# The last gate's 512 rows of the second output product as seven block products of their own, the sixth of them last

## The chip, the cores and the metric

One core of a Trainium2 chip runs the whole program. The time is device microseconds of one execution. Of a run with a profile there is also the span, from the first to the last instruction.

## What is computed

A trunk of two encoder layers over 512 tokens of width 1024, with 256 memory tokens. Each layer projects the normalized input, attends (the first layer with dilated windows, the second with grouped queries), attends to the memory, gates the heads, and multiplies by an output matrix of 1536 x 1024, with a residual. What matters here is the end of the second layer:

```python
        o_mem = memory_attention(q_mem, mem_h, w_mem_kv[i], mem_qn_g[i], mem_kn_g[i])
        y = jnp.concatenate([o_mix, o_mem], axis=-1) * jax.nn.silu(gate)
        x = x + jnp.einsum('bse,ed->bsd', y, w_out[i])
```

`y` is 512 tokens x 1536, `w_out[1]` is 1536 x 1024. All of it is float32.

## The kernel before

**Products of three matmuls.** TensorE takes each float32 operand as two parts, a high one (a cast by ScalarE to `fp32r`) and a low one (the source minus the high part, by VectorE). A product is high x high, low x high (`mm_early`, L176 and L177) and high x low (`mm_late`, L180).

**Seven block products.** Most large products go through `s_chunk` (L388): both operands are cut into 2 x 2 blocks, and seven products of sums of blocks (`PRODUCTS`, L386: "12", "11", "S1", "S2", "S4", "S3", "22") stand for the eight of the plain way. S1 = a21 - a22, S2 = S1 - a11, S4 = a12 + S2, S3 = a11 - a21 are made by VectorE. The weights' sums T1 to T4 are made by DMAs that add on arrival (`Weights.sum`, L277): T1 and T3 load a block on top of another one (L261), T2 adds T1 (L297), T4 adds T2 to block 21 (L307). The results are put together by `keep` (ScalarE copies a bank out of PSUM, L398) and `add` (VectorE adds a bank to a kept one, L415).

**Weights.** `PLAN` (L38) lists the weight chunks by kind, and `Weights` runs ahead of the products: SP loads a piece (128 x 1024) into a tile `wl`, ScalarE makes the high part `wh` (L323), VectorE the low part `wo` (L333). `KEEP` (L45) limits the pieces that are held at a time.

**The end of the second layer.** Three gates follow each other (`gate` in `gates`, L825); the first two make the forms of `y` for 1024 of the 1536 rows of `w_out`, the third (g = 2) makes `y` for the other 512. `out_proj` (L940) first runs the 1024 rows as seven block products of `s_chunk(512, YW, ...)`, 24 matmuls each; the attention of the second layer and the third gate's evaluation run beside the first six of them. `ev` in `out_proj` adds the residual to each quarter of the result `acc` by a DMA on POOL (L953, eight of 128 x 512). Then `out_rest` (L798) does the other 512 rows in the plain way: for each half of the columns (`n`) and each 128 tokens (`b`), twelve matmuls of 512 columns into a bank, VectorE adds the bank to `acc` (L781), and ScalarE's queue stores it (L1584). The last of these eight groups is cut into two of 256 columns (L806, L1592). In it, `y` comes as a high part cast by ScalarE (L880) and a low part by VectorE (L882); the weights are two `O1` chunks of two pieces each.

The order of the work is that of the code: a driver (`Driver`, L48) steps the generators of the evacuations and preparations at ticks between the products, and each engine works off its own queue in the order in which instructions were written.

Of the kernel before, what the change touches and what calls it, by code (L numbers as in the profile page):

```python
# [37 lines left out]
PLAN = ["W2"] + ["T2"] * 2 + ["W1", "W2s"] + ["W2" if c.isdigit() else "W1" for c in A_ORDER[1:]] + ["W2"] + ["O1"] * 2 + ["T2b"] * 2 + ["W1bs", "W2c"] + ["W1b"] * 4 + ["W2b"] + ["O1"] * 2  # L38
# [6 lines left out]
KEEP = {"T2": 8, "T2b": 6, "O1": 6, "W1": 9, "W2": 10, "W2s": 9, "W1bs": 9, "W2c": 9, "W1b": 7, "W2b": 9}  # L45
# [86 lines left out]
def trunk_kernel(ctx: ExitStack, tc: tile.TileContext, x, mem, wall, norm_g, mem_norm_g, gcol,  # L132
# [59 lines left out]
    def pieces(kind):  # L192

        return 2 * GROUPS[kind][0] if kind in GROUPS else 4 if kind in ("W1", "W1b", "W1bs") else 8

    class Weights:
        def __init__(self):
# [3 lines left out]
            for c in SEQ:  # L201
# [23 lines left out]
                else:  # L225
                    n = 1 if kind in ("W1", "W1b", "W1bs") else 2
                    at = {k: [d + i * n + x for x in range(n)] for i, k in enumerate(("21", "11", "12", "22"))}
# [162 lines left out]
    def s_chunk(n, act, ev, tokens=True, pre=None, half=False, soon=False, tight=False, place=None, pairs=False):  # L390
# [3 lines left out]
        bank, snap = [None, None], {}  # L394
# [25 lines left out]
        for i, (a, s, fresh) in enumerate(PRODUCTS):  # L420
            while a not in act:
                drv.tick()
            if fresh:
                bank[s] = [pj() for _ in range(units)]
            for x in range(units):
# [7 lines left out]

                for b, k, kk, bs, o in regions():
                    if half and b and k == per // 2:
                        n_half[0] += 1
                        if n_half[0] % half == 0:
                            drv.half()
                    st = fresh and kk == 0 and (units == 2 or b == 0)
                    if tokens:  # L440
                        mm_early(o, ah[:, kk, bs], wh[:, k], al[:, kk, bs], wh[:, k], st)
                    else:
                        mm_early(o, wh[:, k, bs], ah[:, kk], wh[:, k, bs], al[:, kk], st)
                for b, k, kk, bs, o in regions():
                    if tokens:
                        mm_late(o, ah[:, kk, bs], wo[:, k], kk == 3)
                    else:
                        mm_late(o, wo[:, k, bs], ah[:, kk], kk == 3)
                drv.free()
                W.advance()  # L450
                if x == units - 1:
# [324 lines left out]
    def out_rest(ys, acc, done, evac, last=None):  # L776
# [9 lines left out]
        for bs in ((0, 1), (2, 3)):  # L786
            for n in range(2):
# [5 lines left out]
                for b in bs:  # L793
# [4 lines left out]
                    if last and (n, b) == (1, 3):  # L798
                        assert (n, b) in done
                        for c in range(2):  # L800
                            es = slice(c * 256, c * 256 + 256)
                            for k in range(4):
                                mm_early(p[:, es], ys[k][0][:, cs], w[k][0][:, es], ys[k][0][:, cs], w[k][1][:, es], k == 0)
                            for k in range(4):
                                mm_late(p[:, es], ys[k][1][:, cs], w[k][0][:, es], k == 3)
                            V.tensor_tensor(acc[b][n][:, es], p[:, es], acc[b][n][:, es], ALU.add)  # L806
                            last(n, b, acc[b], c, es)
                            if not c:
                                drv.free()
                                drv.tick()  # L810
                        continue
# [9 lines left out]
    def gates(od, o_done, o_here, direct):  # L821
# [3 lines left out]
        def gate(H, first, g, half=False):  # L825


            yt = [[m4(F32R, "y").rearrange("p (h t) -> p h t", h=2) for _ in range(2)] for _ in range(2)] if g == 2 else None
# [3 lines left out]
            def ev(q, u, t):  # L832
# [46 lines left out]
                yield 1  # L879
                A.copy(yt[j][0][:, :, ts], tv)  # L880
# [57 lines left out]
        return gate, prep_y, YW, ys  # L938

    def out_proj(YW, ys, src, evac, tiles, half=False, last=None):  # L940
# [17 lines left out]
        out_rest(ys, acc, done, evac, last)  # L958
# [616 lines left out]
    gate, prep_y, YW, ys = gates(od_b, o_done_b, o_here_b, DIRECT_B)  # L1575
# [15 lines left out]
    def last_o2(n, b, o, c, es):  # L1591
        (nc.sync if c else nc.scalar).dma_start(ov[b][:, n * 512 + c * 256:n * 512 + c * 256 + 256], o[n][:, es])  # L1592
# [107 lines left out]
```

## Time and profile before

| | |
|---|---|
| Median of 3 runs | 945.94 us (944.49 to 946.8) |
| The profiled execution | 944.79 us |
| Its span | 943.0 us |
| Granted TensorE clock | 1.000 |
| First matmul of `out_rest` | 916.75 us from the span's start |
| Last matmuls of `out_rest` (four at L180) start | 938.95 us |
| Last addition of VectorE | 939.62 to 940.04 us |

Rows of the trace in order of time have the start in us from the span's start, the duration in us, the engine, the line of the kernel, the operation, what it writes and reads, its size and how many rows were merged (`x4`); in brackets stands how long its engine had been idle and what ended that. PE is TensorE, PEld its weight loads, DVE is VectorE, ACT is ScalarE; a q behind the name is the engine's queue, on which DMAs are issued.

### The profile page before, as it was taken

How to read it: one execution, taken by the hardware profiler on the slowest of the kernel's cores; microseconds unless marked ns; L12 is line 12 of the kernel's file. 1: busy time of each engine (PE TensorE's matmuls, PEld its weight loads, DVE VectorE, ACT ScalarE, POOL GpSimd, SP SyncE). 2: the span in 40 equal slices, each digit the busy share in tenths (PEclk: the TensorE clock that was granted, in tenths of full speed). 3: DMA queues.
4: the chain of work that ended last, by engine and by line, in shares of the span. 5: the costliest groups of instructions: out<-in, count | busy, mean ns of one | idle time of the engine just before them, and what ended most of it. 6: DMA issues, size and time to landing. Idle time of an engine off the chain costs nothing.

```text
span 943.0 us, 16294 instructions
## 1 busy us (share of the span) xinstructions
PE 935.4 (99%) x5524; PEld 823.2 (87%) x5524; DVE 790.1 (84%) x1430; ACT 682.9 (72%) x1706; POOL 339.1 (36%) x486
## 2 busy tenths in 40 slices
PE   8999999999999999999999999999999999999998
PEld 6889888888888888888889998888988999999886
DVE  6998676879888888889798999877998997789972
ACT  7775788677768686868676768547879887888860
POOL 3411425455655545464737111214253340110110
PEclk9999999999999999999999999999999999999999
DMA  9999937869786878796967989979985786784824
GB/s 348 386 267 337 289 93 188 279 135 258 159 250 144 262 152 265 158 267 135 254 172 192 262 205 249 290 253 304 277 187 113 189 232 162 209 219 109 199 41 118
DMA packets 87989, 202.96 MB, mean 215 GB/s; under 512 B 25057, under 2 KB 34529, under 8 KB 87906
## 3 DMA queue, kind: packets, MB, share of 16 engines
q1 hardware_dynamic: 68242, 139.07, 43.4%
q0 software_dynamic: 18368, 60.83, 35.0%
q10 hardware_dynamic: 1296, 2.03, 0.6%
q8 instruction: 43, 0.70, 0.3%
q14 instruction: 40, 0.33, 0.1%
HBM read 156.21 MB, written 11.08 MB: 177 GB/s over the span
## 4 chain that ended last, share of the span: by engine, by line
PE 91%; DVE 4%; DMA 3%; ACT 1%; issue 0%; POOL 0%; SPq 0%; DVEq 0%; ACTq 0%; POOLq 0%
PE pj L176 24%; PE pj L177 24%; PE pj L180 23%; DMA wl<-in_wall_dram 3%; PE qT L620 3%; PE sa L1215 2%; PE oo L1323 2%; PE pt L1302 1%; PE ptb L1529 1%; PE sa L1211 1%; PE xT L515 1%; DVE wo L333 1%; PE ob L180 1%; PE ob L177 1%; PE ob L176 1%; PE sb L171 1%
## 5 line engine op out<-in xcount | busy, mean ns | idle before, releaser
L333 DVE TENSOR_TENSOR wo<-wl,wh 128x1024 fp32r<-128x1024 f32 x255 | 312.6, 1232 | 5.5 <-ACT wh L323 5.3
L323 ACT CAST wh<-wl 128x1024 fp32r<-128x1024 f32 x255 | 268.8, 1060 | 32.2 <-PE pj L177 20.5
L176 PE MATMUL pj<-wh,hS 128*128 128x512 f32 (+1 forms) x416 | 154.5, 380 | 0.0
L177 PE MATMUL pj<-wh,hS 128*128 128x512 f32 (+1 forms) x416 | 149.0, 367 | 0.0
L176 PE MATMUL pj<-wh,h 128*128 128x512 f32 (+1 forms) x312 | 115.4, 379 | 0.0
L177 PE MATMUL pj<-wh,h 128*128 128x512 f32 (+1 forms) x312 | 111.7, 367 | 0.0
L463 POOL TENSOR_TENSOR rstd<-mse,half 128x4 f32<-128x4 f32 (+2 forms) x98 | 103.0, 1052 | 8.2
L180 PE MATMUL pj<-wo,hS 128*128 128x512 f32 (+1 forms) x416 | 99.5, 366 | 0.0
L177 PEld LDWEIGHTS pj<-wh,hS 128*128 128x128 f32 x416 | 78.8, 189 | 11.2
L176 PEld LDWEIGHTS pj<-wh,hS 128*128 128x128 f32 x416 | 78.6, 189 | 11.1 <-DVE sn L415 0.2
L180 PEld LDWEIGHTS pj<-wo,hS 128*128 128x128 f32 x416 | 72.5, 189 | 13.1
L462 POOL TENSOR_SCALAR mse<-hss 128x4 f32<-128x4 f32 (+1 forms) x88 | 46.0, 523 | 101.7 <-ACT junk L608 93.9
L608 ACT ACTIVATE junk<-sn 128x128 f32<-128x128 f32 x264 | 79.3, 310 | 3.4 <-DVE sn L409 3.3
L1159 POOL TENSOR_TENSOR ta<-sn,tabs 128x128 f32<-128x128 f32 (+1 forms) x64 | 34.7, 549 | 119.6 <-DVE sn L613 91.8
L398 ACT COPY sn<-pj 128x512 f32<-128x512 f32 x116 | 63.9, 588 | 17.7 <-PE pj L180 16.9
L180 PE MATMUL pj<-wo,h 128*128 128x512 f32 (+1 forms) x312 | 74.5, 366 | 0.0
L307 POOL DMA_DIRECT2D wl<-wl x33 | 29.3, 897 | 109.9 <-DVE wo L333 69.8
L176 PEld LDWEIGHTS pj<-wh,h 128*128 128x128 f32 x312 | 59.0, 189 | 8.4 <-DVE sn L415 0.2
L177 PEld LDWEIGHTS pj<-wh,h 128*128 128x128 f32 x312 | 59.1, 189 | 8.3
L415 DVE TENSOR_TENSOR sn<-pj,sn 128x512 f32<-128x512 f32 x87 | 59.4, 684 | 7.0 <-PE pj L180 6.7
L261 POOL DMA_DIRECT2D wl<-in_wall_dram x38 | 35.9, 963 | 75.2 <-DMA wl<-in_wall_dram 22.3
L180 PEld LDWEIGHTS pj<-wo,h 128*128 128x128 f32 x312 | 54.4, 189 | 9.7
(255 smaller groups left out, 2363.3 us busy)
## 6 DMA issues: line engine op xcount, KB each, us to landing
wl<-in_wall_dram SPq DMA_DIRECT2D x222, 512.0 KB, 7.4
wl<-wl POOLq DMA_DIRECT2D x66, 512.0 KB, 5.6
wl<-in_wall_dram POOLq DMA_DIRECT2D x42, 512.0 KB, 8.5
od<-o SPq DMA_DIRECT2D x11, 256.0 KB, 5.5
og<-od SPq DMA_DIRECT2D x10, 256.0 KB, 8.5
x<-in_x_dram SPq DMA_DIRECT2D x4, 512.0 KB, 9.2
v0d<-sn SPq DMA_DIRECT2D x8, 256.0 KB, 11.3
acc<-in_x_dram POOLq DMA_DIRECT2D x8, 256.0 KB, 7.0
```

The source lines that it names most:

```text
L176: T.matmul(o, a, b, start=start, stop=False, skip_group_check=True)
L177: T.matmul(o, c, d, start=False, stop=False, skip_group_check=True)
L180: T.matmul(o, a, b, start=False, stop=stop, skip_group_check=True)
L261: queue.dma_start(t, wall[d], **how)
L323: A.copy(wh, self.tile[self.items[i]])
L333: V.tensor_tensor(wo, self.tile[key], wh.bitcast(F32), ALU.subtract)
L398: A.copy(t, b)
L415: V.tensor_tensor(t, b, t, ALU.subtract if q == "12" else ALU.add)
L462: G.tensor_scalar(e, ss, EPS, None, ALU.add)
L463: G.tensor_tensor(r, e, half[:, 0:n], ALU.pow)
L608: A.activation(jk, p[:, j * 128:(j + 1) * 128], AF.Square, scale=by, accum_out=ss[:, j:j + 1])
L1159: G.tensor_tensor(ta[:, 0:n], xn[:, 0:n, 0:32], ropeA[:, 0, b, s0:s0 + n], ALU.mult)
```

## The change

In the second layer `out_rest` is no longer called. The third gate leaves its four blocks of `y` as they are (`forms=True`), a new generator `prep_l` makes from them the seven forms for a second `s_chunk`, over 512 rows (`K=2`, so that each product has twelve matmuls), and the two `O1` chunks become one chunk `W1o` of six loads, with sums T1 to T4. In this `s_chunk` the last two products change places: "22", the seventh, goes sixth into banks of its own (`at`), and "S3", the sixth, comes last, cut into one whole bank and two halves of the other. `mid` and `final` add both into what is stored, so that no step stands between S3 and the stores but two operations of VectorE. The functions of the first layer stay as they are.

```diff
-PLAN = [...] + ["W1bs", "W2c"] + ["W1b"] * 4 + ["W2b"] + ["O1"] * 2
+PLAN = [...] + ["W1bs", "W2c"] + ["W1b"] * 4 + ["W2b", "W1o"]
...
-                    for k in ORDER:
+                    for k in ORDER[:5] + ("T4", "T3") if kind == "W1o" else ORDER:
...
-    def s_chunk(n, act, ev, ..., pairs=False):
+    def s_chunk(n, act, ev, ..., pairs=False, K=4, tail=None):
...
+            if name == "s5" and tail:
+                tail[0](u, t)
...
+        def mid(u, b):
+            t = snap["21", u] = s2(name="sn")
+            tail[1](u, t, b)
+            yield 1
+
+        if tail:
+            after = after[:5] + ((mid,),)
-        for i, (a, s, fresh) in enumerate(PRODUCTS):
+        for i, (a, s, fresh) in enumerate(PRODUCTS[:5] + (("22", 2, True), ("S3", 1, False)) if tail else PRODUCTS):
...
-                bank[s] = [pj() for _ in range(units)]
-            for x in range(units):
+                bank[s] = [(at if s == 2 else pj)() for _ in range(units)]
+            for x in range(K // per):
...
+                if tail and i == 6:
+                    for b, c in ((0, slice(0, 512)), (1, slice(0, 256)), (1, slice(256, 512))):
+                        o, ts = bank[s][b][:, c], slice(b * 128, (b + 1) * 128)
+                        for k in range(per):
+                            mm_early(o, ah[:, k, ts], wh[:, k, c], al[:, k, ts], wh[:, k, c], False)
+                        for k in range(per):
+                            mm_late(o, ah[:, k, ts], wo[:, k, c], k == per - 1)
...
+                        tail[2](b, snap["21", b], snap["s5", b], o, c)
+                    continue
...
+                if forms:
+                    ys[2 * j + i] = t
+                    return
                 A.copy(yt[j][0][:, :, ts], tv)
...
+        def prep_l():
+
+            def put(k, src):
+                t = m4(F32R, "yl" + k)
+                A.copy(t[:, 0:512], src)
+                drv.late(lambda: V.tensor_tensor(t[:, 512:1024], src, t[:, 0:512].bitcast(F32), ALU.subtract))
+                YL[k] = t.rearrange("p (a k t) -> p a k t", a=2, k=2)
...
+            put("12", ys[2])
...
+            put("11", ys[0])
...
+            V.tensor_tensor(s1, a21, a22, ALU.subtract)
+            put("S1", s1)
+            yield 1
+            V.tensor_tensor(s2_, s1, a11, ALU.subtract)
+            put("S2", s2_)
+            yield 1
+            V.tensor_tensor(a12, a12, s2_, ALU.add)
+            put("S4", a12)
+            yield 1
+            V.tensor_tensor(a21, a11, a21, ALU.subtract)
+            put("S3", a21)
+            yield 1
+            put("22", a22)
...
-        out_rest(ys, acc, done, evac, last)
+        if not last:
+            out_rest(ys, acc, done, evac)
+            return
+        prep_l, YL = ys
+        drv.spawn(prep_l())
+
+        def ev_l(q, u, t):
...
+            V.tensor_tensor(acc[b][n], t, acc[b][n], ALU.add)
+            yield 1
+            yield from evac(n, b, acc[b])
+
+        def sum_22(u, t):
...
+            V.tensor_tensor(t, t, acc[2 + u][1], ALU.add)
+
+        def sum_21(u, t, p):
...
+            V.tensor_tensor(t, p, acc[2 + u][0], ALU.add)
+
+        def final(u, t, t22, p, c):
+            V.tensor_tensor(t[:, c], p, t[:, c], ALU.add)
+            last(0, 2 + u, t, c)
+            V.tensor_tensor(t22[:, c], t22[:, c], p, ALU.subtract)
+            last(1, 2 + u, t22, c)
+
+        s_chunk(512, YL, ev_l, tight=True, K=2, tail=(sum_22, sum_21, final))
...
-    gate, prep_y, YW, ys = gates(od_b, o_done_b, o_here_b, DIRECT_B)
+    gate, prep_y, YW, ys = gates(od_b, o_done_b, o_here_b, DIRECT_B, True)
...
+    def last_o2(n, b, t, c):
+        (nc.sync if n else nc.scalar).dma_start(ov[b][:, n * 512 + c.start:n * 512 + c.stop], t[:, c])
```

Up to the last product of the 1024 rows each queue keeps its order, but for the third gate's casts (ScalarE) and subtractions (VectorE), which are gone, and for loads and sums of weights. In what follows the lines of before and of the changed kernel differ by the change: L415 of before is L417 now, L409 is L411, L953 is L999.

VectorE at the end of the program, before, from the evacuation of the large product's last bank on (`pj` are banks of PSUM, `acc` the result with the residual, `wo` the low part of weights):

```order
L415 TENSOR_TENSOR acc<-pj,acc 128x512
L333 TENSOR_TENSOR wo<-wl,wh 128x1024
L415 TENSOR_TENSOR acc<-pj,acc 128x512
L781 TENSOR_TENSOR acc<-pj,acc 128x512
L333 TENSOR_TENSOR wo<-wl,wh 128x1024
L781 TENSOR_TENSOR acc<-pj,acc 128x512 x5
L806 TENSOR_TENSOR acc<-pj,acc 128x256
L781 TENSOR_TENSOR acc<-pj,acc 128x512
L806 TENSOR_TENSOR acc<-pj,acc 128x256
```

VectorE of the changed kernel from the same place on (`yl` and `ylS` are forms of `y` with their low part at L955, or a block sum at L970 and L973; `sn` are blocks of `y` or kept results):

```order
L417 TENSOR_TENSOR acc<-pj,acc 128x512 x2
L333 TENSOR_TENSOR wo<-wl,wh 128x1024
L955 TENSOR_TENSOR yl_11515<-sn,yl_11515 128x512
L333 TENSOR_TENSOR wo<-wl,wh 128x1024
L970 TENSOR_TENSOR yl<-sn 128x512
L955 TENSOR_TENSOR ylS_11543<-yl,ylS_11543 128x512
L417 TENSOR_TENSOR sn<-pj,sn 128x512 x2
L333 TENSOR_TENSOR wo<-wl,wh 128x1024
L973 TENSOR_TENSOR yl<-yl,sn 128x512
L955 TENSOR_TENSOR ylS_11569<-yl,ylS_11569 128x512
L333 TENSOR_TENSOR wo<-wl,wh 128x1024
L976 TENSOR_TENSOR sn<-sn,yl 128x512
```

Where one evacuation a product stood, there now stand a block sum, a low part of the form, a low part of the weights and the evacuations. The queue goes on with two L1014, the low part of S4, a low part of weights, L979, two L1020 (the additions to block 22), and then:

```order
L955 TENSOR_TENSOR ylS_11616<-sn,ylS_11616 128x512
L955 TENSOR_TENSOR yl_11623<-sn,yl_11623 128x512
L417 TENSOR_TENSOR sn<-pj,sn 128x512 x2
L1024 TENSOR_TENSOR sn<-at,acc 128x512
L1014 TENSOR_TENSOR acc<-sn,acc 128x512 x2
L1024 TENSOR_TENSOR sn<-at,acc 128x512
L1027 TENSOR_TENSOR sn<-pj,sn 128x512
L1029 TENSOR_TENSOR sn<-sn,pj 128x512
L1027 TENSOR_TENSOR sn<-pj,sn 128x256
L1029 TENSOR_TENSOR sn<-sn,pj 128x256
L1027 TENSOR_TENSOR sn<-pj,sn 128x256
L1029 TENSOR_TENSOR sn<-sn,pj 128x256
```

The low part of form 22, of which the sixth product has need, now stands behind all of this, and two operations of VectorE follow each piece of the seventh.

TensorE's last matmuls before, the two halves of the last group, with the engine whose semaphore an instruction waits for:

```order
L176 MATMUL pj<-wh,y 128x256 [waits DVE_49]
L177 MATMUL pj<-wo,y 128x256
L176 MATMUL pj<-wh,y 128x256
L177 MATMUL pj<-wo,y 128x256
L176 MATMUL pj<-wh,y 128x256
L177 MATMUL pj<-wo,y 128x256
L176 MATMUL pj<-wh,y 128x256
L177 MATMUL pj<-wo,y 128x256
L180 MATMUL pj<-wh,y 128x256 x4
```

And in the changed kernel, the last product's two half banks:

```order
L176 MATMUL pj<-wh,ylS_11616 128x256
L177 MATMUL pj<-wh,ylS_11616 128x256
L176 MATMUL pj<-wh,ylS_11616 128x256
L177 MATMUL pj<-wh,ylS_11616 128x256
L180 MATMUL pj<-wo,ylS_11616 128x256 x2
L176 MATMUL pj<-wh,ylS_11616 128x256 [waits DVE_49]
L177 MATMUL pj<-wh,ylS_11616 128x256
L176 MATMUL pj<-wh,ylS_11616 128x256
L177 MATMUL pj<-wh,ylS_11616 128x256
L180 MATMUL pj<-wo,ylS_11616 128x256 x2
```

The second half still waits for VectorE's reads of the first, and a half has six matmuls where it had twelve.

More of the change, by code (lines that the diff above doesn't have):

```diff
@@ L225, in __init__ @@
                 else:
[L226 to L227 removed]
+                    n = 1 if kind in ("W1", "W1b", "W1bs", "W1o") else 2
+                    at = {k: [d + i * n + x for x in range(n)] for i, k in enumerate(("11", "21", "12", "22") if kind == "W1o" else ("21", "11", "12", "22"))}
                     if kind == "W2c":
@@ L774, in mem_attn, with out_rest @@
                             (0, top, 1), (1, recip, 1), (4, hi, 1), (4, lo, 1), (6, out_, 1), step=step)
-    def out_rest(ys, acc, done, evac, last=None):
+    def out_rest(ys, acc, done, evac):
         def ev(n, b, p):
@@ L797, in out_rest @@
                     p = pj()
[L798 to L811, printed above, removed]
                     for k in range(4):
```

43 lines of the change are left out of this document (30 added, 13 removed).

## The prediction

> **What bounds the kernel now.** I begin with the page: the busy shares, then the chain that ended last.
>
> ```profile
> PE 935.4 (99%) x5524; PEld 823.2 (87%) x5524; DVE 790.1 (84%) x1430; ACT 682.9 (72%) x1706; POOL 339.1 (36%) x486
> ...
> PE 91%; DVE 4%; DMA 3%; ACT 1%; issue 0%; POOL 0%; SPq 0%; DVEq 0%; ACTq 0%; POOLq 0%
> ```
>
> TensorE is busy all the time and is the chain. The change touches the tail alone, so I cut the end into three stretches: most of the large output product, its last part, and the plain product of the last gate's rows (from 916.75). Columns are each engine's busy time, then granted clock, DMA share, GB/s.
>
> ```profile
> 863.00:890.00 27.00, 27.00 (x147) 23.14 (x146) 26.33 (x47) 22.87 (x43) 3.95 (x5) 1.00 0.68 139
> 890.00:916.75 26.75, 26.75 (x140) 22.70 (x140) 21.53 (x33) 19.61 (x32) 3.20 (x4) 1.00 0.34 97
> 916.75:943.00 26.25, 22.32 (x109) 18.64 (x107) 8.90 (x13) 0.34 (x1) 2.06 (x3) 1.00 0.45 120
> ```
>
> Up to 916.75 TensorE has no idle time. Behind it VectorE works 8.90 of 26.25 us and ScalarE almost nothing: that is the room into which the change puts work. Then TensorE's rows in order of time, from the last matmuls of the large product on.
>
> ```profile
> 915.84 1.07 PE L180 MATMUL pj<-wo,y 128*128 128x512 f32 x4
> 916.75 0.39 PE L176 MATMUL pj<-wh,y 128*128 128x512 f32 x1
> ...
> 919.47 0.39 PE L176 MATMUL pj<-wh,y 128*128 128x512 f32 x1
> ...
> 935.79 0.28 PE L176 MATMUL pj<-wh,y 128*128 128x256 f32 x1
> ...
> 937.89 0.39 PE L176 MATMUL pj<-wh,y 128*128 128x256 f32 x1 [0.52 <-DVE acc L806]
> 938.12 0.28 PE L177 MATMUL pj<-wo,y 128*128 128x256 f32 x1
> 938.24 0.28 PE L176 MATMUL pj<-wh,y 128*128 128x256 f32 x1
> ...
> 938.95 0.64 PE L180 MATMUL pj<-wh,y 128*128 128x256 f32 x4
> ```
>
> A group of twelve 512-column matmuls takes 919.47 - 916.75 = 2.72 us, 0.227 us each from start to start; one ends 0.39 us after its start. At 256 columns a step is 0.12 us, and the first step behind a wait 0.23. The only wait is at 937.89: the second half of the last group writes the PSUM bank whose first half VectorE still reads.
>
> VectorE's rows of the same stretch, and the last store.
>
> ```profile
> 914.25 1.29 DVE L409 TENSOR_TENSOR acc<-acc 128x512 f32<-128x512 f32 x2
> 916.49 0.69 DVE L415 TENSOR_TENSOR acc<-pj,acc 128x512 f32<-128x512 f32 x1 [0.96 <-PE pj L180]
> 917.10 1.22 DVE L333 TENSOR_TENSOR wo<-wl,wh 128x1024 fp32r<-128x1024 f32 x1
> 918.24 0.68 DVE L415 TENSOR_TENSOR acc<-pj,acc 128x512 f32<-128x512 f32 x1
> ...
> 937.42 0.42 DVE L806 TENSOR_TENSOR acc<-pj,acc 128x256 f32<-128x256 f32 x1 [3.46 <-PE pj L180]
> 937.76 0.68 DVE L781 TENSOR_TENSOR acc<-pj,acc 128x512 f32<-128x512 f32 x1
> 939.62 0.42 DVE L806 TENSOR_TENSOR acc<-pj,acc 128x256 f32<-128x256 f32 x1 [1.18 <-PE pj L180]
> ```
> ```profile
> 940.07 0.34 SPq L1592 DMA_DIRECT2D out_dram<-acc  x1
> ```
>
> One VectorE operation occupies the engine (start to start) for 0.60 us at 512 columns (916.49 to 917.10; the pair at 914.25, SBUF alone, lasts 1.29 = 0.60 + 0.69), 1.14 at 1024 (917.10 to 918.24) and 0.34 at 256 (937.42 to 937.76). The last one ends at 940.04, and the span ends 2.96 us later: store, landing, closing waits.
>
> **The change part by part.**
>
> *TensorE.* Eight groups of twelve become seven products of twelve: 12 x 0.227 = 2.72 us less.
>
> *Ahead of the tail.* Four casts on ScalarE go, each like this one from SBUF, and four subtractions on VectorE.
>
> ```profile
> 884.36 0.63 ACT L880 CAST y<-sn 128x512 fp32r<-128x512 f32 x1
> ```
>
> They lay beside a TensorE without idle time, so they are worth nothing. The large product keeps its order on TensorE, so the first of the seven products can still start at 916.75, and VectorE still starts its first evacuation of the large product's last bank at 916.49.
>
> *Behind 916.49 on VectorE.* By the order of the change it now has, in 512-column operations, 6 evacuations at L417, 6 low parts (L955; the seventh is done earlier), 4 block sums (L970 to L979), 8 additions of parts (L1014, L1020, L1024) and the 2 whole ones of the end (L1027, L1029): 26 x 0.60 = 15.6 us. Five low parts of weights are 5 x 1.14 = 5.7, four quarter pieces 4 x 0.34 = 1.4. Together 22.7 us against 8.90 before and against 19.0 us of matmuls. **VectorE becomes the bound**, so the tail has to be walked along its queue.
>
> Two of its low parts wait for ScalarE in a round trip: the block sum ends, ScalarE casts it, VectorE subtracts the cast. Such a handover is seen at the start of the program.
>
> ```profile
> 11.99 0.59 ACT L164 CAST act<-xT 128x512 fp32r<-128x512 f32 x1 [1.15 <-PE xT L515]
> ...
> 12.61 0.69 DVE L167 TENSOR_TENSOR act<-xT,act 128x512 fp32r<-128x512 f32 x1 [0.75 <-ACT act L164]
> ...
> 13.35 0.50 PE L177 MATMUL pj<-wh,act 128*128 128x512 f32 x1 [0.23 <-DVE act L167]
> ...
> 13.69 0.39 PE L176 MATMUL pj<-wh,act 128*128 128x512 f32 x1
> ```
>
> ScalarE ends at 12.58 and VectorE starts at 12.61: 0.03 us. VectorE ends at 13.30 and the matmul that needs the low part starts at 13.35: 0.05, and its next one 0.34 later instead of 0.23. So from the start of a block sum to the start of its low part: 0.69 + 0.03 + 0.63 (the cast of L880) + 0.03 = 1.38 us, 0.78 more than its slot (the way from VectorE to ScalarE taken as 0.03 too). This hits S1 and S2, whose sum and low part are neighbours in the queue; for S4 and S3 two operations stand between.
>
> The walk: from 916.49 up to the low part of form 22 stand 17 operations of 512 columns (10.2), 5 of 1024 (5.7) and two round trips (1.56): it starts at 933.95 and ends at 934.64. TensorE's sixth product waits for it at its second matmul: 934.69, next at 935.03; the bank of the first 128 tokens is complete with the tenth matmul, 7 x 0.227 later plus 0.39: 937.01. Without waits the sixth product would have started at 916.75 + 5 x 2.72 = 930.35. VectorE has meanwhile evacuated the fifth and is free from 935.75. From 937.05: L1024, two L1014, L1024 (2.4), L1027 and L1029 whole (1.2), L1027 and L1029 on the first quarter piece, the last of which starts at 940.99 and ends at 941.41.
>
> The last quarter piece of TensorE goes to the bank that these two have read, and by the order it waits for VectorE: start 941.46, six matmuls (0.23, then 4 x 0.12, then 0.28 for the last to end): 942.45. Then L1027 at 942.49, L1029 at 942.83, its end 943.25. Before, this end was 940.04: **+3.2 us**. The store behind it is of the same size as before, so 2.96 us follow again.
>
> [...] By addresses alone VectorE would run straight on (941.33 and 941.67, end 942.09), and the sum would be +2.05.
>
> Unknown costs, by bounds:
> - Two stores now stand on ScalarE's queue ahead of the cast of form 22. The group of output stores has
>
> ```profile
> L1584 ACTq DMA_DIRECT2D out_dram<-acc x7: 338/339/461, 920.4 to 938.7; - x7
> ```
>
>   so 0.7 to 0.9 us. The cast of S3 starts at 932.27 by the walk, that of 22 then at 933.0 to 933.3 and ends at 933.6 to 933.9, when VectorE wants it: 0 to 0.1 us. I take 0.
> - The weights of the last 512 rows now come as six loads, with four sums made by DMAs on POOL, T1 to T2 to T4 in series. Before, SP issued the last loads, and POOL sums landed, as follows.
>
> ```profile
> 867.08 24.92 SPq L261 DMA_DIRECT2D wl<-in_wall_dram  x7
> ```
> ```profile
> wl<-in_wall_dram SPq DMA_DIRECT2D x7, 512.0 KB, 4.1
> ...
> wl<-in_wall_dram POOLq DMA_DIRECT2D x2, 512.0 KB, 7.0
> wl<-wl POOLq DMA_DIRECT2D x1, 512.0 KB, 5.2
> ```
>
>   Seven loads end at 892.0, 3.6 us apart. Two more: 899.2 (an estimate from these rows). The T2 load, third from the end, is then out at 892.0 and landed at 896.1; T1's sum at about 899.5 (888.4 + 4.1 + 7.0), T2's at 904.7. It is cast at 916.04 at the earliest. T4 needs also the low part of block 21 (about 911.3): landed at 916.9, cast behind 921. Cost 0, with 4 us and more to spare; if the spare goes, every late us of T4 is a late us of the end.
> - The eight additions of x1d stand on POOL between these sums; the first that VectorE waits for anew is L1014 at about 928.6. Cost 0.
> - How exact is the walk? Some 35 slots at 0.60 +- 0.01 and a dozen handovers at 0.03 to 0.10: -0.4 to +0.9 us. I take 3.2 as it stands.
>
> The span goes from 943.0 to 946.2, this execution from 944.79 to 948.0. The median of the three runs is 945.94, 1.15 above the profiled execution, so the forecast for the median is 945.94 + 3.2 = **949.1 us** (+0.34%).
>
> **The rivals.**
> - *VectorE keeps up, and the saved matmuls show: faster.* Then TensorE runs through: the last piece but one is complete at 935.24, two reads of it until 936.04, the last piece 936.09 to 937.08, VectorE until 937.88: 2.2 us ahead of 940.04, **943.8**. It decides at the low part of form 22: this would have to be there by 930.35 and not 934.64, which takes 512-column slots of about 0.44 us. For it speaks that VectorE is idle for 0.96 us ahead of 916.49; against it that slots are 0.60 whether an operand is in PSUM or not, and that the queue's order leaves that work behind. Chance 0.04.
> - *The weight sums are late.* If SP gets its buffers later than I think, or the three sums in series take the double, T4 comes 2 to 5 us late: about **952.5**. For it: POOL's sums wait behind each other and behind x1d additions. Against: the spare above. Chance 0.05.
> - *The clock drops when TensorE waits.* A second slower step of 0.45 us on the matmuls of the path (seven of the sixth product, five quarter steps) adds 1.6 + 0.6: **951.3**. Against it: the granted clock is 1.00 in all stretches, and the longest new gap of TensorE is 1.9 us (939.6 to 941.46). Chance 0.03. [...]
> - The change doesn't do what it says: the order shows the twelve matmuls gone, so this is out.
>
> **How the numbers follow.** The forecast has 0.88, the rivals 0.04, 0.05, 0.03. About 0.3% (2.8 us) is what a measurement of this kernel can tell from no change. The forecast's +3.2 lies just over that bound; with its -0.4 to +0.9 and some 0.6 us for medians of runs that spread over 2.3 us, about 0.7 of its chance falls above: 0.60 slower, 0.27 within, 0.01 faster. With the rivals: 0.60 + 0.05 + 0.03 = 0.68 slower, 0.27 within, 0.01 + 0.04 = 0.05 faster. The range takes the forecast with its errors and part of the late sums: 947.2 to 951.2.
>
> **What would show it.** In the changed profile the first product of the last gate starts near 916.75; VectorE is busy nearly without idle time from there to about 935.8, with two gaps of some 0.7 us ended by ScalarE; TensorE waits in the products of S1, S2, S4 and 22, each time for VectorE or ScalarE, some 4 us in all, and some 2 us at the last piece. The stretch behind 916.75 has 22 to 23 us of VectorE. Wrong would be: waits of ScalarE for DMA ahead of a weight cast (sums late), matmul steps of 0.45 (clock), or slots of VectorE under 0.6.

## The result, and the profile after

The changed kernel takes 948.85 us (median of eight, 947.11 to 950.7), the kernel before, timed beside it, 944.71 us (median of eight, 944.31 to 946.8). The ratio is 1.004, with a 95% interval of 1.0028 to 1.0052: slower by 0.4%. The profiled execution of the changed kernel took 947.53 us, its span is 945.7 us.

First the page's busy times and chain, to be read against those of before.

```profile
PE 933.9 (99%) x5506; PEld 819.8 (87%) x5506; DVE 802.3 (85%) x1449; ACT 691.1 (73%) x1718; POOL 343.4 (36%) x490
...
PE 93%; DVE 4%; ACT 1%; DMA 1%; issue 0%; SPq 0%; DVEq 0%; ACTq 0%
```

Over 946 us hardly anything shows: 1.5 us less on TensorE, 12.2 more on VectorE, 8.2 more on ScalarE. The stretches tell more; the columns are those of before (busy time of each engine with its instructions, granted clock, DMA share, GB/s).

```profile
890.00:916.75 26.75, 26.75 (x139) 22.65 (x138) 19.86 (x29) 19.43 (x32) 7.07 (x8) 1.00 0.80 186
916.75:945.70 28.95, 20.96 (x90) 15.43 (x88) 22.49 (x35) 9.60 (x16) 1.80 (x3) 0.96 0.43 109
```

Ahead of 916.75 nothing has moved for TensorE: it is full, and with the weights' extra loads and sums the DMAs' rate nearly doubles (186 GB/s against 97). Behind it TensorE has fewer matmuls (18 less in the whole kernel: twelve, and six of the piece that is cut), and VectorE has gone from 8.90 to 22.49 us. TensorE's rows say where it waits.

```profile
916.42 0.39 PE L176 MATMUL pj<-wh,yl 128*128 128x512 f32 x1
...
921.89 0.39 PE L176 MATMUL pj<-wh,ylS 128*128 128x512 f32 x1
922.36 0.50 PE L177 MATMUL pj<-wh,ylS 128*128 128x512 f32 x1
...
925.94 0.51 PE L176 MATMUL pj<-wh,ylS 128*128 128x512 f32 x1 [0.80 <-ACT ylS L954]
926.67 0.51 PE L177 MATMUL pj<-wh,ylS 128*128 128x512 f32 x1 [0.22 <-DVE ylS L955]
...
930.22 0.50 PE L177 MATMUL pj<-wh,ylS 128*128 128x512 f32 x1 [0.52 <-DVE ylS L955]
...
933.48 0.50 PE L176 MATMUL at<-wh,yl 128*128 128x512 f32 x1 [0.48 <-ACT yl L954]
934.36 0.50 PE L177 MATMUL at<-wh,yl 128*128 128x512 f32 x1 [0.38 <-DVE yl L955]
...
936.99 0.39 PE L176 MATMUL pj<-wh,ylS 128*128 128x512 f32 x1
...
941.14 0.39 PE L176 MATMUL pj<-wh,ylS 128*128 128x256 f32 x1 [1.92 <-DVE sn L1029]
941.36 0.28 PE L177 MATMUL pj<-wh,ylS 128*128 128x256 f32 x1
```

Where before there was one wait of 0.52 us, there are now waits in the products of S2, S4 and 22, each for ScalarE's cast or VectorE's low part, and 1.92 us at the last quarter piece. The second matmul of S1's product comes 0.47 us behind the first instead of 0.23, so it waits too, without a bracket. The six products up to the last take 20.57 us (916.42 to 936.99) where six times 2.72 are 16.32: 4.2 us of waiting in all. Now VectorE, from the block sum S1 to its end.

```profile
920.24 0.69 DVE L970 TENSOR_TENSOR yl<-sn 128x512 f32<-128x512 f32 x1
921.62 0.69 DVE L955 TENSOR_TENSOR ylS<-yl,ylS 128x512 fp32r<-128x512 f32 x1 [0.69 <-ACT ylS L954]
922.22 1.28 DVE L417 TENSOR_TENSOR sn<-pj,sn 128x512 f32<-128x512 f32 x2
923.42 1.22 DVE L333 TENSOR_TENSOR wo<-wl,wh 128x1024 fp32r<-128x1024 f32 x1
924.55 0.69 DVE L973 TENSOR_TENSOR yl<-yl,sn 128x512 f32<-128x512 f32 x1
925.92 0.69 DVE L955 TENSOR_TENSOR ylS<-yl,ylS 128x512 fp32r<-128x512 f32 x1 [0.68 <-ACT ylS L954]
...
933.62 0.69 DVE L955 TENSOR_TENSOR yl<-sn,yl 128x512 fp32r<-128x512 f32 x1
934.22 1.28 DVE L417 TENSOR_TENSOR sn<-pj,sn 128x512 f32<-128x512 f32 x2
936.73 0.69 DVE L1024 TENSOR_TENSOR sn<-at,acc 128x512 f32<-128x512 f32 x1 [1.23 <-PE at L180]
...
940.67 0.41 DVE L1029 TENSOR_TENSOR sn<-sn,pj 128x256 f32<-128x256 f32 x1
942.15 0.43 DVE L1027 TENSOR_TENSOR sn<-pj,sn 128x256 f32<-128x256 f32 x1 [1.07 <-PE pj L180]
942.49 0.41 DVE L1029 TENSOR_TENSOR sn<-sn,pj 128x256 f32<-128x256 f32 x1
```

Brackets are what to look for: from the tail's start on this queue has four gaps, two round trips to ScalarE (0.69 and 0.68) and two waits for TensorE, which itself had waited for VectorE. Everything else follows start to start at 0.60, 1.14 or 0.34 us.

In what follows **the tail** is the time from the first matmul of the last gate's rows to the end of VectorE's last operation. It went from 23.29 us (916.75 to 940.04) to 26.48 (916.42 to 942.90). The span ends 2.82 us behind it (2.94 before, by the span unrounded).

### The profile page after: what moved, and what is told of

It is laid out like the page before. It is cut to its first block, busy times and chain, and to the rows that moved or that the text cites. A ratio compares the mean times of both kernels' runs of the same rounds, so it can differ in the third digit from the quotient of the medians.

```text
span 945.7 us, 16305 instructions
## 1 busy us (share of the span) xinstructions
PE 933.9 (99%) x5506; PEld 819.8 (87%) x5506; DVE 802.3 (85%) x1449; ACT 691.1 (73%) x1718; POOL 343.4 (36%) x490
## 4 chain that ended last, share of the span: by engine, by line
PE 93%; DVE 4%; ACT 1%; DMA 1%; issue 0%; SPq 0%; DVEq 0%; ACTq 0%
PE pj L176 24%; PE pj L177 24%; PE pj L180 24%; PE qT L641 3%; PE sa L1289 2%; PE oo L1397 2%; PE ptb L1603 1%; PE pt L1376 1%; PE sa L1285 1%; DVE wo L333 1%; PE xT L536 1%; PE ob L180 1%; PE ob L177 1%; PE ob L176 1%; PE sb L171 1%; PE sb L170 1%
## 5 line engine op out<-in xcount | busy, mean ns | idle before, releaser
L333 DVE TENSOR_TENSOR wo<-wl,wh 128x1024 fp32r<-128x1024 f32 x258 | 316.2, 1232 | 6.7 <-ACT wh L323 6.5
L323 ACT CAST wh<-wl 128x1024 fp32r<-128x1024 f32 x258 | 272.0, 1060 | 31.9 <-PE pj L177 20.9
L398 ACT COPY sn<-pj 128x512 f32<-128x512 f32 x122 | 67.2, 590 | 19.3 <-PE pj L180 18.5
L417 DVE TENSOR_TENSOR sn<-pj,sn 128x512 f32<-128x512 f32 x91 | 62.0, 684 | 7.1 <-PE pj L180 6.6
L261 POOL DMA_DIRECT2D wl<-in_wall_dram x40 | 38.1, 969 | 82.2 <-DMA wl<-in_wall_dram 30.1
```

The source lines that it names most:

```text
L261: queue.dma_start(t, wall[d], **how)
L323: A.copy(wh, self.tile[self.items[i]])
L333: V.tensor_tensor(wo, self.tile[key], wh.bitcast(F32), ALU.subtract)
L417: V.tensor_tensor(t, b, t, ALU.subtract if q == "12" else ALU.add)
```

## The experiments

The theory after the result is that of the prediction: VectorE's queue sets the tail, and the last wait for a bank adds to it. Its rivals are the weights' sums (late), the handovers between VectorE and ScalarE (their latency, not the slots), and the new order of the last two products. Executions of one kernel spread by 2 to 4 us here, so the verdicts go by the tail, read from each trace.

| Kernel | first matmul | tail | span behind it | time, us |
|---|---|---|---|---|
| before | 916.75 | 23.29 | 2.94 | 944.71 (8) |
| change | 916.42 | 26.48 | 2.82 | 948.85 (8) |
| no sums of weights | 917.69 | 26.47 | 2.83 | 948.77 |
| no sums of `y` | 918.57 | 23.76 | 2.83 | 946.93 |
| two sums made twice | 917.28 | 27.97 | 2.84 | 949.86 |
| usual order | 916.93 | 27.10 | 3.48 | 949.27 |
| last piece whole | 918.24 | 25.21 | 3.50 | 948.72 |
| operands early | 917.46 | 26.08 | 3.53 | 948.83 |
| additions on GpSimd | 916.07 | 29.33 | 2.84 | 950.01 |
| early, whole, GpSimd | 917.38 | 25.48 | 4.09 | 948.46 (6) |
| additions by DMA | 918.12 | 25.35 | 3.54 | 948.77 |
| early, whole, DMA | 917.59 | 22.88 | 4.24 | 945.95 (11) |
| before again | 917.32 | 23.31 | 2.95 | 945.35 |
| the same, stores earlier | 917.42 | 22.66 | 3.50 | 945.58 (11) |

Medians have their number of executions behind them, the others are one execution. Each tail is read from one profile.

**No sums of weights.** For the last chunk T1 to T4 become plain loads, or a name for one.

```diff
+            if self.sums and PLAN[self.sums[0][0][0]] == "W1o":
+                if key[1] == "T4":
...
+                    self.tile[key] = self.tile[key[0], "21", key[2]]
```

> The sums T1 to T4 of the last gate's weights are left out: the four pieces are used as they were loaded, so that the four DMAs that add are gone from POOL (the output of the last gate's rows is then not the reference's). I measure the tail, from the first matmul of the last gate's rows to the end of VectorE's last operation: 23.29 us in the kernel before, 26.48 in the changed one. Theory V (VectorE's queue is the bound): the tail stays at 26.5, within 0.1. Theory S (the sums of the weights or their DMAs come late and hold TensorE): the tail shrinks by 2 to 3 us, to 23.5 to 24.5. Theory H (the handovers between VectorE and ScalarE are the cost): 26.5.

The tail is 26.47 us, as in the change. The sums cost nothing; that rival is out.

**No sums of `y`.**

```diff
-            V.tensor_tensor(s1, a21, a22, ALU.subtract)
-            put("S1", s1)
+            put("S1", a21)
...
-            V.tensor_tensor(a12, a12, s2_, ALU.add)
             put("S4", a12)
```

> The four block sums S1, S2, S4 and S3 of the last gate's y are left out: the forms are cast from single blocks (the output of the last gate's rows is then not the reference's). Casts, low parts and everything else stay. Theory V: 4 slots of 0.60 and two round trips of 0.78 go from VectorE's queue ahead of the low part of form 22, 3.9 us; TensorE's seven products (5 x 2.72 up to the sixth) then stand close behind, so the tail shrinks by 2.7 us, to 23.8. Theory H: the two round trips go, 1.5 us: 25.0. Theory S: 26.5.

23.76: 2.72 us less, the number that was expected, but not by the way that was expected. Both round trips were to go, and TensorE was to be the bound. In the trace only S2's round trip is gone (0.78 us of the queue); the low part of S1 now waits longer for its cast, which stands behind other work of ScalarE:

```profile
923.61 0.69 DVE L955 TENSOR_TENSOR ylS<-sn,ylS 128x512 fp32r<-128x512 f32 x1 [1.13 <-ACT ylS L954]
...
933.77 0.50 PE L177 MATMUL at<-wh,yl 128*128 128x512 f32 x1 [0.52 <-DVE yl L955]
```

That is 0.44 us more than in the change (1.13 against 0.69). So four slots of 0.60 make 2.40, and the handovers together 0.34. TensorE's sixth product still waits for VectorE's low part: VectorE's queue stays the bound, and the slots are most of what counts. The theory of the handovers had 25.0.

**Two sums made twice.** One more operation ahead of S1's and S2's form each.

```diff
             V.tensor_tensor(s1, a21, a22, ALU.subtract)
+            V.tensor_tensor(s1, a21, a22, ALU.subtract)
```

> VectorE makes the block sums S1 and S2 twice, one after the other into the same tile; the result is unchanged. This adds two operations of 512 columns to VectorE's queue and no wait. Theory V: each slot ahead of the low part of form 22 is paid in full: the tail grows by 1.2 to 1.4 us, to 27.7 to 27.9. Theory S or a bound of TensorE: the tail stays at 26.5.

27.97: 1.49 us for two operations, about 0.75 each. The slot is 0.60; the repeated operation, which writes the same tile, starts 0.72 behind the first (921.10 to 921.82 in the trace), 0.12 more than a slot. Every slot ahead of form 22 reaches the end of the kernel.

**The usual order.** S3 sixth, 22 last, all of it through `add` and `keep` as in other products.

```diff
-        s_chunk(512, YL, ev_l, tight=True, K=2, tail=(sum_22, sum_21, final))
+        s_chunk(512, YL, ev_l, tight=True, K=2)
```

> The seven products of the last gate's rows in the usual order, S3 sixth and 22 last, with the usual evacuations: the second half of the change is undone, the first stays. Theory V: the work on VectorE in front of the last two products is nearly the same, but behind the last product there now stand two evacuations and four additions of the result instead of two operations, and no bank wait: by the slots the tail is 27.1 us, 0.6 longer than with 22 sixth, and 3.8 longer than before the change. Rival B (the order with the cut last product and its bank wait is what costs): the tail is shorter than 26.5, 24 to 25.

27.10 us: the changed order is worth 0.6 us, so it isn't what made the kernel slower.

**The last piece whole.**

```diff
-                    for b, c in ((0, slice(0, 512)), (1, slice(0, 256)), (1, slice(256, 512))):
+                    for b, c in ((0, slice(0, 512)), (1, slice(0, 512))):
```

> The last product's second bank comes in one piece of 512 columns instead of two of 256, so that no matmul goes to a bank that VectorE still has to read; VectorE then has two operations of 512 columns at the end instead of four of 256. Theory that the end is VectorE's queue plus one wait for the bank: VectorE's last four quarter operations (4 x 0.34) and the wait between them go, two of 0.60 come; the tail (first matmul of the last gate's rows to the end of VectorE's last operation, 26.48 us in the change, 23.29 before) becomes 25.3. Theory that VectorE is the bound in throughput alone and the order at the end costs nothing: 26.2 to 26.5.

25.21 us, 1.27 less: the wait for the bank was a cost of its own. But the span now ends 3.50 us behind VectorE instead of 2.82, with last stores twice as large and the DMAs at 377 to 385 GB/s from 943 to 945: half of the gain is given back.

**Operands early.** `prep_l` starts ahead of the large product.

```diff
+        if last:
+            prep_l, YL = ys
+            drv.spawn(prep_l())
         s_chunk(512, YW, ev, half=half, tight=True, place=place)
...
-        prep_l, YL = ys
-        drv.spawn(prep_l())
```

> The generator that makes the operands of the last products (casts, low parts, block sums) is started ahead of the first products of the other gates instead of behind them, so that its first casts and low parts run where VectorE still has idle time. Theory that VectorE's queue behind the start of the tail is the bound: whatever of it goes ahead of the start comes off the tail; by the order of the instructions that is about 1 us: 25.5. Theory that the operands' handovers (ScalarE's cast, then VectorE's low part) set the end and not the queue: 26.4, since the block sums keep their place behind each other.

26.08, between the two, so the number alone decides nothing. TensorE's rows at the last piece say why, and the stretches around it, with the granted clock third from the end.

```profile
941.09 0.58 PE L176 MATMUL pj<-wh,ylS 128*128 128x256 f32 x1 [2.93 <-DVE sn L1030]
941.48 0.42 PE L177 MATMUL pj<-wh,ylS 128*128 128x256 f32 x1
941.69 0.41 PE L176 MATMUL pj<-wh,ylS 128*128 128x256 f32 x1
```
```profile
936.00:940.00 4.00, 2.16 (x13) 1.72 (x11) 4.00 (x8) 0.00 (x0) 0.00 (x0) 1.00 0.17 66
940.00:940.80 0.80, 0.00 (x0) 0.00 (x0) 0.80 (x3) 0.00 (x0) 0.00 (x0) 0.65 0.15 59
940.80:943.00 2.20, 1.65 (x6) 1.36 (x6) 0.46 (x2) 0.00 (x0) 0.00 (x0) 0.50 0.91 336
```

TensorE now comes to the last piece earlier and waits 2.93 us for the bank, and meanwhile the granted clock falls to half. The steps are 0.39 and 0.21 us instead of 0.22 and 0.12, and from the piece's first matmul to VectorE's next operation it takes 1.69 us (941.09 to 942.78) where the change took 1.01 (941.14 to 942.15). Without these 0.68 us the tail would be 25.40, the 25.5 of the queue theory.

**Additions on GpSimd.**

```diff
-            V.tensor_tensor(acc[b][n], t, acc[b][n], ALU.add)
+            G.tensor_tensor(acc[b][n], t, acc[b][n], ALU.add)
...
-            V.tensor_tensor(t, t, acc[2 + u][1], ALU.add)
+            G.tensor_tensor(t, t, acc[2 + u][1], ALU.add)
```

> Six additions of finished parts (the four of L1014 and the two of L1020, 128x512 each) go from VectorE to GpSimd, which has 1.8 us of work in this stretch. Theory that VectorE's queue is the bound: six slots of 0.60 go from the queue, but not all stand ahead of the low part of form 22 or of the end; with GpSimd at an estimated 1.25 us for one of them (worked out from its 0.5 to 0.75 us at 64 to 128 columns) the tail becomes about 25.1. If GpSimd takes over 3 us for each, they land too late for the output and the tail stays at 26.5 or gets longer. Theory that handovers are the bound: 26.5.

29.33: neither theory had a tail 2.85 us longer. GpSimd's rows of this kernel, and VectorE's beside the first of them:

```profile
922.65 3.48 POOL L1014 TENSOR_TENSOR acc<-sn,acc 128x512 f32<-128x512 f32 x2 [4.00 <-DVE sn L417]
927.89 3.53 POOL L1020 TENSOR_TENSOR sn<-sn,acc 128x512 f32<-128x512 f32 x2 [1.76 <-ACT sn L398]
938.08 2.54 POOL L1014 TENSOR_TENSOR acc<-sn,acc 128x512 f32<-128x512 f32 x2 [6.65 <-DVE sn L417]
```
```profile
921.88 1.28 DVE L417 TENSOR_TENSOR sn<-pj,sn 128x512 f32<-128x512 f32 x2
923.08 1.94 DVE L333 TENSOR_TENSOR wo<-wl,wh 128x1024 fp32r<-128x1024 f32 x1
924.94 1.75 DVE L973 TENSOR_TENSOR yl<-yl,sn 128x512 f32<-128x512 f32 x1
927.37 0.69 DVE L955 TENSOR_TENSOR ylS<-yl,ylS 128x512 fp32r<-128x512 f32 x1 [0.68 <-ACT ylS L954]
927.97 2.31 DVE L333 TENSOR_TENSOR wo<-wl,wh 128x1024 fp32r<-128x1024 f32 x1
930.21 1.76 DVE L976 TENSOR_TENSOR sn<-sn,yl 128x512 f32<-128x512 f32 x1
```

Two additions take GpSimd 2.54 us where VectorE has little to do (busy for 1.31 of them), 1.27 each, close to the estimate of 1.25; beside VectorE they take 3.5. And VectorE's own operations, 0.69 and 1.22 us elsewhere, take 1.75, 1.94 and 2.31: four of them lose 3.9 us in all, while the four additions ahead of form 22 that left the queue were worth 2.4. All four (L333 twice, L973, L976) read two tiles of SBUF; L417, which reads one input from PSUM, keeps its 0.60 step beside the start of GpSimd's first addition (922.65, within the pair at 921.88, which takes 1.28 as elsewhere).

**All three.** The edits of the last three experiments together.

> All three edits together: last piece whole, operands made early, six additions on GpSimd. Theory that VectorE's queue is the bound: the gains add up nearly whole, the tail becomes 22.5 us (change 26.48, before 23.29), so that the seven products beat the kernel before by 0.5 to 1.1 us: 944.0 where the kernel before has 944.7. If something else bounds it once the queue is shorter (ScalarE's casts, GpSimd), the tail stays above 24 and the kernel is slower than before.

25.48 and 948.46 us (ratio to before 1.0038, 1.0025 to 1.0051): in time no better than the change (948.85), though the tail is 1.00 us shorter. VectorE's operations beside GpSimd's additions are stretched as in the run before, to 1.76 to 2.32 us, so this is the second case of its expectation.

**Additions by DMA.** To tell whether it was GpSimd's work or only the additions' lateness, the same six are left to DMAs that add.

```diff
-            V.tensor_tensor(acc[b][n], t, acc[b][n], ALU.add)
+            G.dma_start(acc[b][n], t, accum_op=ALU.add)
...
-            V.tensor_tensor(t, t, acc[2 + u][1], ALU.add)
+            G.dma_start(t, acc[2 + u][1], accum_op=ALU.add)
```

> The same six additions as in the run before with GpSimd (four of L1014, two of L1020), but made by DMAs that add into the target (issued by GpSimd, as the x1d additions of L999), so that GpSimd computes nothing. The run with GpSimd's own additions ended at a tail of 29.33 us, with VectorE's operations beside them stretched from 0.69 to 1.75 us. Theory that GpSimd's and VectorE's operations hinder each other: with DMAs VectorE's operations keep their 0.69 and 1.22 us, six slots go from its queue, and the tail becomes about 25.0 (change 26.48). Theory that the additions were late, or that their order was the trouble: the DMAs take longer than GpSimd did (4 to 5 us from issue to landing), so the tail stays at 27 or more.

VectorE's groups of this kernel in the tail, with mean ns at the end:

```profile
L333 DVE TENSOR_TENSOR wo<-wl,wh 128x1024 fp32r<-128x1024 f32 x5 | 6.1, 1216 | 0.0
...
L973 DVE TENSOR_TENSOR yl<-yl,sn 128x512 f32<-128x512 f32 x1 | 0.7, 685 | 0.0
L976 DVE TENSOR_TENSOR sn<-sn,yl 128x512 f32<-128x512 f32 x1 | 0.7, 684 | 0.0
```

The same operations are back at 1.22 and 0.69 us, the tail is 25.35 against 29.33, though a DMA takes 3.8 us from issue to landing. So it was the two engines' hindering each other, not lateness: the 3.98 us between the two tails are what the four stretched operations lost (3.9). Six slots (3.6 us) brought 1.13 against the change: with the additions gone, S4 and S3 have round trips that wait 0.69 us each, as S1 and S2, and VectorE waits 0.24 for the cast of form 22 and 0.53 for TensorE's last product.

**Early, whole, and four additions by DMA.** A trial for a version that beats both kernels.

```diff
-            V.tensor_tensor(acc[b][n], t, acc[b][n], ALU.add)
+            if q == "11":
+                G.dma_start(acc[b][n], t, accum_op=ALU.add)
+            else:
+                V.tensor_tensor(acc[b][n], t, acc[b][n], ALU.add)
```

The other edits are those shown for operands early, the whole piece, and block 22's additions by DMA.

> Operands made early, last piece whole, and four of the six additions (the first two of L1014 and the two of L1020) by DMAs that add; the last two additions of L1014 stay on VectorE, since a DMA would land them after the rest of the output. Theory that VectorE's queue is the bound: the tail becomes 22.9 us (change 26.48, before 23.29), the kernel level with the one before or up to 0.5 us faster: 944.3 to 945.5. If the DMAs disturb VectorE or the stores at the end, the tail stays above 24 and the time above 946.

The tail is 22.88, as worked out, and TensorE's waits are down to two (0.85 and 0.42 us). Yet the time is 945.95, 1.0013 of before (1.0004 to 1.0022). The stretches around VectorE's end at 940.47 show it in the last two columns, DMA share and GB/s:

```profile
937.00:940.00 3.00, 1.72 (x8) 1.10 (x6) 3.00 (x6) 0.00 (x0) 0.00 (x0) 1.00 0.37 143
940.00:943.00 3.00, 0.00 (x0) 0.00 (x0) 0.47 (x1) 0.00 (x0) 0.00 (x0) 1.00 0.99 378
```

The queue is no longer the end; the output is. Six pieces of 256 KB become ready within some 4 us, and from 940 on the DMAs move them at 378 GB/s without a pause. In the kernel before, the same output trickles out with each group of twelve matmuls (seven stores at L1584 from 920.4 to 938.7 us).

**Before again.** The kernel before, unchanged.

> The kernel before, profiled once more, for the spread of what stands ahead of the tail. The start of the last gate's products was 916.75 in the first profile of before and 916.07 to 918.57 in the changed kernels, whose code up to about 867 us is the same. Theory that the start moves from run to run by waits for DMAs of the unchanged part: here it lies anywhere in 916 to 918.6, and the tail is 23.3 again (23.2 to 23.4). Theory that the change delays the start: 916.7 again.

Tail 23.31, first matmul at 917.32. The start moves without any change. One wait that comes and goes stands in code that is the same in all kernels:

```profile
539.44 0.95 PE L1302 MATMUL pt<-ident,p 128*128 128x128 f32 x7 [0.45 <-DVE p L1289]
```

It is in this profile of before and not in the first one, and in eight of the twelve profiles of changed kernels. Compared matmul by matmul with the first profile of before, TensorE runs at a fixed distance in each of the other thirteen, within 0.05 us, from 600 us up to the first matmul of the tail. The distances, -0.67 to +1.82 us, come about in the first 150 us, at this wait and between 560 and 590 us. On all five engines the instructions and their order are the same in all kernels up to 879 us, so nothing that the change does near the end moves the start.

**The same, stores earlier.** As the trial above, with the last two additions and their stores ahead.

```diff
-            yield 1
+            if not (tail and q == "12"):
+                yield 1
             yield from ev(q, u, t)
...
                 G.dma_start(acc[b][n], t, accum_op=ALU.add)
+                yield 1
             else:
                 V.tensor_tensor(acc[b][n], t, acc[b][n], ALU.add)
-            yield 1
             yield from evac(n, b, acc[b])
```

> As the run before (operands made early, last piece whole, four additions by DMA), but the two additions of L1014 that are left on VectorE come right behind their evacuations, and their stores are issued right behind them, ahead of the last products' stores on ScalarE's queue. In the run before, VectorE ended 0.4 us earlier in its tail than in the kernel before (22.88 against 23.29), but the span went on for 4.24 us behind it (2.96 before): from 940 to 943 the DMAs moved 377 GB/s without a pause, and one store of 256 KB that was ready at 938.1 was issued at 940.29. Theory that this last stretch is bound by the rate of the output's DMAs: with that store ahead of the stretch, a quarter of a MB less is left in it, 0.69 us, the span ends 3.5 us behind VectorE's last operation, the tail stays at 22.8, and the time is 945.1 to 945.4, within 0.1% of the kernel before. Theory that the end behind VectorE is a fixed latency of the last store: 4.2 us again, 945.9.

Tail 22.66 and 3.50 us behind it, as the theory of the DMAs' rate has it; its span behind the first matmul is 26.16 us, that of before 26.23 and 26.26. The time is 945.58, 1.0009 of before (1.0000 to 1.0018), 0.2 above what was expected. That is 3.3 us under the change, and no version is faster than the kernel before.

## Why the prediction was right, point by point

- *Twelve matmuls less on TensorE, 2.72 us, and none of it gained*: so it came. Its busy time behind 916.75 fell from 22.32 to 20.96 us, and the waits, 4.2 us in the first six products (in those of S1, S2, S4 and 22, as forecast) and 1.92 at the last piece, took more back.
- *VectorE becomes the bound with 22.7 us*: 22.49 us behind 916.75. Taking its sums out or doubling them moved the end by 0.68 to 0.75 us an operation, the 0.60 of a slot with what the handovers add, which shows it.
- *The walk along its queue*: from the first matmul, the low part of form 22 was to start 17.20 us later and started 17.20 later (933.62 - 916.42); the last quarter piece 24.71, measured 24.72; VectorE's end 26.50, measured 26.48. S1's and S2's round trips were to cost 0.78 each over their slot; from the start of the sum to the start of its low part the rows have 1.38 and 1.37 us (920.24 to 921.62, 924.55 to 925.92), 0.78 and 0.77 over 0.60. The brackets say 0.69 and 0.68, since an operation lasts 0.09 longer than its slot. Each part agrees, so this is no luck.
- *The bank's wait at the last piece*: 1.92 us at 941.14, behind VectorE's L1029. One piece without this wait took 1.27 off the tail. So the longer of the two sums, +3.2, was the right one; the shorter, by addresses alone, is in no run. The wait is for a semaphore of the program (`waits DVE_49` in its order), as is the one of 0.52 us at 937.89 before, so the runs show its price, not what would come of leaving it out.
- *Unknown costs taken as nothing*: right in all three. The two stores on ScalarE's queue (0.83 us) ended just ahead of the cast of form 22, and that cast, done at 933.43, ahead of VectorE's turn at 933.62, as these rows show. Without the weights' sums the tail was the same to 0.01 us; in the changed profile the sums of T1 and T2 were issued at 894.45 and 902.65, 2 to 3 us later than I had them (892.5 and 899.5), inside the spare. (T4's landing by my numbers is 911.3 + 5.2 = 916.5 and not 916.9, which changes nothing.) No operation of VectorE waited for an x1d addition.

```profile
931.93 0.62 ACT L954 CAST ylS<-sn 128x512 fp32r<-128x512 f32 x1 [1.80 <-DVE sn L979]
931.94 0.83 ACTq L1658 DMA_DIRECT2D out_dram<-acc  x2
932.81 0.62 ACT L954 CAST yl<-sn 128x512 fp32r<-128x512 f32 x1 [0.26 <-issue]
```

- *The rivals*: VectorE kept no pace, since no slot was shorter than 0.60; the sums were in time. *The clock that drops when TensorE waits* I gave 0.03, and with 2.2 us too high a price, but a part of it is true. In the change's profile the clock held until the last matmul, behind a wait of 1.92 us (1.00 up to 943.2, the last matmul over by 942.12); with operands early it fell during the wait of 2.93 us, to 0.50, and cost 0.68. The eight executions of the change have mean clocks of 0.997 to 0.999 where those of before beside the trials have 1.000 in all but two, which have 0.999. By an estimate from the mean and from the 0.50 that these profiles have behind the fall, 0.997 (0.9965 to 0.9975) of 947 us is half speed for the last 4.7 to 6.6 us, which begins ahead of the last piece (4.6 us from the end of the span): three of the eight executions. They took 948.83 to 949.59, the two at 0.998 took 948.80 and 950.70, those at 0.999 took 947.11 to 949.12. These overlap, so the clock's share of the time is not shown.
- *From the span to the median*: 949.1 was forecast and 948.85 came, and that they are so close is luck, since two errors cancel. I counted +3.2 on a median of three, 945.94, which by eight executions was 1.2 too high. And the change ran 1.3 above its own profiled execution, so that the medians differ by 4.1, not 3.2. The step that failed is the last one of the working, that the median lies 1.15 us above the profile after the change as before it: it lay 0.08 below before and 1.3 above after. The span itself grew by 2.7 us and not by 3.2, as the profiled execution of the change started its tail 0.33 earlier (916.42 against 916.75) and ended 0.12 sooner behind VectorE. Of the missing 0.9 us the clock may be one part, in some executions, by the estimate above. Another is the start of the tail: 916.42 in the profiled execution of the change is the second earliest of the twelve profiles of changed kernels (916.07 to 918.57). The same holds for the 1 us by which the last trial stays behind although its tail is shorter: its profile and the second one of before, which start at 917.42 and 917.32, took 945.36 and 945.35 us, so with equal starts the two kernels are level. How often the start is late with the change and without it stays open; two profiles of before are too few to say.
- *Slower by over 0.3%, chance 0.68*: the interval, 0.28 to 0.52%, holds the bound at its lower end.

## What to carry to other kernels

Work that a shorter product scheme takes from TensorE comes back as sums, low parts and evacuations of another engine; count them as slots of its queue in the stretch where they fall, find the one operation for which TensorE waits last, and add the round trips. Where the queue is then relieved, ask what stands behind it: here it was first a wait for a bank (1.92 us), then the rate at which the output leaves (378 GB/s), all of it ready at once. Here a GpSimd that stood idle was not free help for a busy VectorE (tail 29.33 against 26.48), while DMAs that add took time off (25.35).

## What the runs showed of the hardware that I had not expected

GpSimd's additions from SBUF stretched VectorE's to 1.75 us (0.69 alone) and 2.31 (1.22 alone), and were themselves 1.75 instead of 1.27. A DMA that adds, issued by GpSimd, held that engine for 0.9 us and left VectorE's durations as they were (0.69 and 1.22).

The granted clock fell after different spells without matmuls: with operands early 2.1 us behind the end of the last one (938.16 to 940.24, the point worked out from the 0.65 of that stretch), in the kernel before about 4 us behind (0.82 in 943 to 944, the last matmul over by 939.6), in the change 1.3 us behind (942.12 to 943.39, 0.74 in 943.2 to 943.6). With the additions on GpSimd TensorE waited 2.58 us (924.80 to 927.38), and the clock stayed up (1.00 in 900 to 940). So in these runs the length of one spell does not tell when the clock falls, and a wait of 2.93 us was not safe. In the traces of before and of the change the record of full clock begins 11.8 and 11.6 us into the span; matmuls of 512 columns just ahead of that step at 0.43 us, those from 13.7 us on at 0.23. It ends 931.84 us later in both, though the last matmul is over by 939.6 in the one and by 942.12 in the other. What sets the moment of the fall is not shown.
